# Tree attention on one core: the root part of V copied by GpSimd, loads ahead of stores in the DMA queue, the last pair split by heads

## The chip, the cores and the metric

One Trainium2 chip, one core of it. The metric is the device time of one execution in microseconds (us); lower is better. The kernel before was run three times: median 138.92 us, from 138.73 to 139.44.

## What is computed

Attention for 8 x 12 = 96 heads of 512 tokens and 64 dimensions, with a mask in which token i sees itself and its ancestors in a binary tree (the parent of i is (i - 1) // 2):

```python
mask = np.zeros((seq, seq))
for i in range(seq):
    mask[i, i] = 1
    parent = i
    while parent > 0:
        parent = (parent - 1) // 2
        mask[i, parent] = 1
scores = np.einsum('bhqd,bhkd->bhqk', Q, K) * scale
scores = scores + (1 - mask) * (-1e9)
weights = np.exp(scores - np.max(scores, axis=-1, keepdims=True))
weights = weights / (np.sum(weights, axis=-1, keepdims=True) + 1e-10)
return np.einsum('bhqk,bhkd->bhqd', weights, V).astype(np.float32)
```

Inputs and output are float32 in HBM, 12.6 MB each.

## The kernel before

The work is cut into 48 pairs of heads; pair i holds heads 2i and 2i + 1. Token 4p + t of a head lies on partition p, slot t, so a load puts 1 KB of each head on every partition, and the load itself turns float32 into bf16.

For each pair: `transpose` (L237) turns K and Q with 16 small TensorE operations into the PSUM tile `kqp` (one buffer, pool `psT`). `evac` (L250) copies it to SBUF on VectorE. `scores1` and `scores2` (L266, L288) write two groups of masked scores to PSUM (the first group holds keys near the root, the mask comes in through a matmul of codes), and ScalarE takes the exponential of each. `values` (L320) multiplies by V into the PSUM tile `ob`, with a column of ones for the sums of weights. `norm` (L345) takes reciprocals (L351) and multiplies (L352) on VectorE into the output tile `of`, one for two pairs (four heads).

`values` needs V in another order of nodes. So for each group o of 16 heads, V is copied from the loaded tile `vst` into one of two tiles `vt`, by three kinds of copies that all stand on L198: `spread_top` (nodes under 128, four copies, partitions 0 to 31 of the source), `spread_l7` (the next 128 nodes, four copies) and `spread_leaves` (the other 256, two). `vst` has three buffers of 16 heads, the tiles `kst` and `qst` have four buffers of 8 heads.

The order of the work is written out by hand; each engine runs its instructions in the order of the program. In loop step i come the scores of pair i, values and norm of pair i - 1, transposes and evacuation of pair i + 2, then `spread(i)` (L422), which deals out the copies of V, then `pool(i)` (L444). Copies of the first two groups are listed by step in `early` (L397); later groups follow a cycle of eight steps.

All loads and nearly all stores are issued by GpSimd (POOL), in one list, `pool_program` (L366). `pool(i)` takes operations from its front as long as `ready` (L386) lets them go, so a load that has to wait for a buffer holds up everything behind it. Each of these transfers uses one of eight semaphores in turn, so the ninth waits for the landing of the first. A whole transfer of 8 heads of one input is 512 KB on the chip, and so is a store of four heads. Of the copies of V, POOL makes `spread_top` of heads 0 to 7. The output of the last two pairs goes out by SyncE and ScalarE in three stores (L478 to L481).

At the start TensorE runs 21 matmuls on zeros (`fill`, L310), so that it is busy before the first data come.

Of the kernel before, what the change touches and what calls it, by code (L numbers as in the profile page):

```python
# [98 lines left out]
def kernel(  # L99
# [7 lines left out]
    nc = tc.nc  # L107
# [32 lines left out]
    opool = ctx.enter_context(tc.tile_pool(name="opool", bufs=14))  # L140
# [82 lines left out]
    def transpose_one(dst, i, a, t, units, st, perm):  # L223

        step = units[1] - units[0]
        if units[2] - units[1] == step:
            dst = dst[64 * a:64 * a + 64, units[0]:units[3] + 1:step, :]
        else:
            gap = units[2] - units[0]
            dst = dst[64 * a:64 * a + 64, units[0]:units[0] + 2 * gap, :].rearrange(  # L230
                "p (x y) c -> p x y c", x=2
            )[:, :, 0:2, :]
        nc.tensor.transpose(  # L233
            out=dst, in_=st[2 * i // KB][:, 2 * i % KB + a, t, :], identity=perm
        )
# [84 lines left out]
    def values(i):  # L320

        if i not in obs:
            obs[i] = psO.tile([P, 2, 512], fp32, name="ob")
        ob = obs[i]
        e1, e2, vt = ets[i], e2s[i % NE], vts[(2 * i // VB) % NV]

        def product(e, a, t, tile_v, lo=0, hi=128, **flags):
            nc.tensor.matmul(  # L328
                out=ob[lo:hi, a, 65 * t:65 * t + 65],
                lhsT=e[:, a, PLACE[t], lo:hi],  # L330
                rhs=vt[:, 2 * i % VB + a, tile_v, 0:D + 1],
                **flags,
            )

        for a in range(2):
            for t in range(4):
                product(e1, a, t, 0, start=t == 0, stop=False)
            for t in (2, 3):
                product(e2, a, t, 1 + t, start=False, stop=False)
        for a in range(2):  # L340
            for t in (0, 1):
                product(e2, a, t, 1 + SELF[t], 0, 64, start=False, stop=t == 1)
                product(e2, a, t, 1 + t, 64, 128, start=False, stop=t == 1)

    def norm(i):  # L345
        q, r = divmod(i, 2)
        if r == 0:
            ofs[q] = opool.tile([P, 4, 4, D], fp32, name="of")
        o4 = obs[i][:, :, 0:260].rearrange("p a (t c) -> p a t c", c=D + 1)
        rec = small.tile([P, 2, 4, 1], fp32, name="rec")  # L350
        nc.vector.reciprocal(out=rec[:, :, :, :], in_=o4[:, :, :, D:D + 1])  # L351
        nc.vector.tensor_tensor(  # L352
            out=ofs[q][:, 2 * r:2 * r + 2, :, :],
            in0=o4[:, :, :, 0:D],
            in1=rec[:, :, :, :].to_broadcast([P, 2, 4, D]),
            op=ALU.mult,
        )
# [8 lines left out]
    def pool_program():  # L366

        def tops(h0, h1):
            return [(spread_top, nc.gpsimd, j, 0, h0, h1) for j in range(4)]
# [5 lines left out]
        ops += [(load_v, 8, 8), (load_qk, 8, 4)] + tops(0, 4) + [(load_qk, 12, 4)] + tops(4, 8)  # L375
        ops += [(load_qk, 16, 8), (load_v, 16, 8), (load_v, 24, 8), (load_qk, 24, 8)]
        ops += [(load_v, 32, 8), (load_v, 40, 8), (load_qk, 32, 8)]
        ops += [(load_v, 48, 8), (load_v, 56, 8), (load_qk, 40, 8)]
        for g, qs in ((6, (0,)), (7, (1,)), (8, (2, 3)), (9, (4, 5))):
            ops += [(load_v, 8 * g + 16, 8), (load_qk, 8 * g, 8)] + stores(*qs)  # L380
        ops += [(load_qk, 80, 4)] + stores(6, 7) + [(load_qk, 84, 4)] + stores(8, 9)
        ops += [(load_qk, 88, 4)] + stores(10, 11, 12) + [(load_qk, 92, 2)] + stores(13, 14)
        ops += [(load_qk, 94, 2)] + stores(*range(15, NQ - 1))
        return ops

    def ready(op, i):  # L386
# [4 lines left out]
        if f is load_v:  # L391
            return i >= (-1, -1, -1, 3, 11, 15)[args[0] // VB]
        if f is spread_top:
            return True
        return 2 * i >= 4 * (args[1] + 1)

    def early(i):  # L397
# [3 lines left out]
        top = lambda ks, o, h0, h1: [(spread_top, v, k, o, h0, h1) for k in ks]  # L401
        leaf = lambda ks, o, h0, h1: [(spread_leaves, s, k, o, h0, h1) for k in ks]
        if i == 0:
            return l7(range(4), 0, 0, 4) + leaf((0, 1), 0, 0, 4)
        if i == 1:
            return l7(range(4), 0, 4, 8) + leaf((0, 1), 0, 4, 8)
        if i == 2:
            return top(range(4), 0, 8, 16)
        if i == 3:
            return l7(range(4), 0, 8, 16) + leaf((0, 1), 0, 8, 16)  # L410
        if i in (6, 7, 8):
            h = (0, 8)
        elif i in (9, 10, 11):
            h = (8, 16)
        else:
            return []
        n = i % 3
        return [top(range(3), 1, *h) + leaf((0,), 1, *h),
                top((3,), 1, *h) + l7((0, 1), 1, *h) + leaf((1,), 1, *h),
                l7((2, 3), 1, *h)][n]  # L420

    def spread(i):  # L422

        if i < 12:
            todo = early(i)
        else:
            v, s = nc.vector, nc.scalar
            o, k = divmod(i + 7, 8)
            if o < 2 or o >= NH // VB:
                todo = []  # L430
            else:
                top = [(spread_top, v, j) for j in range(4)]
                l7 = [(spread_l7, v, j) for j in range(4)]
                leaf = [(spread_leaves, v, 0)] + [(spread_leaves, s, 1, h, h + 8) for h in (0, 8)]
                todo = [top[:2], top[2:], leaf[:2], l7[:1], l7[1:2] + leaf[2:], l7[2:3], l7[3:], []]
                if o == 2:
                    todo = [[], [], [], top[:3], top[3:] + leaf[:2], l7[:2] + leaf[2:], l7[2:], []]
# [21 lines left out]
    fill(0, 4)  # L459
# [4 lines left out]
    for i in range(1, NP + 1):  # L464
# [3 lines left out]
        if i >= 2:  # L468
            values(i - 1)
            norm(i - 1)  # L470
# [41 lines left out]
```

## Time and profile before

| What | Value |
|---|---|
| median of three runs | 138.92 us |
| the profiled execution | 139.43 us |
| its span | 136.6 us |
| TensorE (PE) busy | 115.4 us, 85% |
| VectorE (DVE) busy | 108.1 us, 79% |
| ScalarE (ACT) busy | 100.9 us, 74% |
| GpSimd (POOL) busy | 62.7 us, 46% |
| DMA packets | 41737, 32.06 MB |

The profile shows one execution. Its page gives the busy time of each engine, the span in 40 equal slices of 3.4 us (a digit 9 is 90% or more; for the DMA it is the mean of 16 DMA engines), and the chain of work that ended last, followed back from the last instruction. The view of transfers gives, for the DMAs issued in a stretch, how long they took from issue to landing. The difference of 2.8 us between the execution's time and its span lies around the program.

### The profile page before, as it was taken

How to read it: one execution, taken by the hardware profiler on the slowest of the kernel's cores; microseconds unless marked ns; L12 is line 12 of the kernel's file. 1: busy time of each engine (PE TensorE's matmuls, PEld its weight loads, DVE VectorE, ACT ScalarE, POOL GpSimd, SP SyncE). 2: the span in 40 equal slices, each digit the busy share in tenths (PEclk: the TensorE clock that was granted, in tenths of full speed). 3: DMA queues.
4: the chain of work that ended last, by engine and by line, in shares of the span. 5: the costliest groups of instructions: out<-in, count | busy, mean ns of one | idle time of the engine just before them, and what ended most of it. 6: DMA issues, size and time to landing. Idle time of an engine off the chain costs nothing.

```text
span 136.6 us, 5453 instructions
## 1 busy us (share of the span) xinstructions
PE 115.4 (85%) x2420; PEld 79.6 (58%) x2421; DVE 108.1 (79%) x220; ACT 100.9 (74%) x116; POOL 62.7 (46%) x84
## 2 busy tenths in 40 slices
PE   6999867795998968779999999999998999879820
PEld 2345545573675646557676766666765667657510
DVE  3344997869879999989999899999899988665440
ACT  4083977659799898568997879996879977785900
POOL 6997987323420362342262253342446746644200
PEclk9999999999599999999999999999999999999995
DMA  3999999999999999999999999999999999999972
GB/s 88 143 156 193 197 196 201 194 200 196 197 198 198 198 199 199 197 198 197 276 201 200 279 198 225 326 204 212 333 299 278 330 281 359 337 354 404 354 303 91
DMA packets 41737, 32.06 MB, mean 235 GB/s; under 512 B 1226, under 2 KB 38730, under 8 KB 41714
## 3 DMA queue, kind: packets, MB, share of 16 engines
q0 software_dynamic: 40960, 30.94, 125.1%
q1 hardware_dynamic: 560, 0.56, 1.2%
q8 instruction: 18, 0.29, 0.8%
q10 hardware_dynamic: 194, 0.23, 0.6%
q14 instruction: 5, 0.04, 0.1%
HBM read 38.01 MB, written 12.58 MB: 370 GB/s over the span
## 4 chain that ended last, share of the span: by engine, by line
DMA 56%; PE 23%; POOL 6%; ACT 6%; issue 4%; DVE 1%; POOLq 0%; ACTq 0%
DMA vst<-in_V_dram 44%; DMA out_dram<-of 11%; PE ob L328 8%; PE kqp L233 5%; PE s L270 3%; PE s L293 3%; POOL kst L185 2%; ACT e L304 2%; POOL qst L185 2%; PE s L299 2%; PE s L275 2%; ACT e L281 2%; ACT vt L198 2%; POOL vt L198 1%; DVE of L352 1%
## 5 line engine op out<-in xcount | busy, mean ns | idle before, releaser
L281 ACT ACTIVATE e<-s 128x1024 bf16<-128x1024 f32 x48 | 49.1, 1024 | 25.8 <-PE s L275 25.2
L328 PE MATMUL ob<-vt,e 128*128 128x65 bf16 (+1 forms) x960 | 38.6, 198 | 6.9 <-DVE of L352 6.0
L328 PEld LDWEIGHTS <-e 128*128 128x128 bf16 (+1 forms) x960 | 30.5, 103 | 15.2 <-DVE of L352 6.5
L304 ACT ACTIVATE e<-s 128x768 bf16<-128x768 f32 x48 | 38.6, 804 | 0.0
L198 DVE COPY vt<-vst 32x1024 bf16<-32x1024 bf16 (+3 forms) x68 | 35.1, 516 | 3.2 <-DMA vst<-in_V_dram 1.9
L259 DVE COPY kq<-kqp 128x1024 bf16<-128x1024 bf16 x48 | 32.7, 682 | 4.9 <-PE kqp L233 4.9
L352 DVE TENSOR_TENSOR of<-ob,rec 128x512 f32<-128x512 f32 x48 | 33.2, 692 | 1.7
L360 POOL DMA_DIRECT2D out_dram<-of x23 | 18.3, 797 | 20.1 <-DVE of L352 8.1
L185 POOL DMA_DIRECT2D kst<-in_K_dram x18 | 15.0, 833 | 14.9 <-DMA kst<-in_K_dram 5.5
L270 PE MATMUL s<-ctile 40*128 40x512 bf16 x96 | 19.2, 394 | 2.9 <-ACT e L281 2.6
L233 PE MATMUL kqp<-ptile,kst 128*64 128x128 bf16 x384 | 19.4, 223 | 1.7 <-issue 0.9
L185 POOL DMA_DIRECT2D qst<-in_Q_dram x18 | 15.1, 839 | 12.3 <-PE kqp L233 3.9
L233 PE MATMUL kqp<-ptile,qst 128*64 128x128 bf16 x384 | 19.5, 223 | 0.8 <-DMA qst<-in_Q_dram 0.8
L299 PEld LDWEIGHTS <-kq 64*128 64x128 bf16 x384 | 14.5, 94 | 8.8 <-issue 1.0
L185 POOL DMA_DIRECT2D vst<-in_V_dram x13 | 11.4, 882 | 17.8 <-DVE rec L351 6.6
L275 PE MATMUL s<-kq 64*128 64x512 bf16 x96 | 18.7, 383 | 1.0 <-DVE kq L259 1.0
L351 DVE RECIPROCAL rec<-ob 128x8 f32<-128x8 f32 x48 | 9.9, 205 | 12.1 <-PE ob L328 11.4
L293 PE MATMUL s<-ctile 40*128 40x480 bf16 x96 | 17.9, 368 | 0.8 <-ACT e L304 0.3
L198 ACT COPY vt<-vst 64x1024 bf16<-64x1024 bf16 (+1 forms) x18 | 17.0, 946 | 1.7 <-DMA vst<-in_V_dram 1.4
L299 PE MATMUL s<-kq 64*128 64x64 bf16 (+1 forms) x384 | 17.7, 209 | 0.4 <-issue 0.4
L233 PEld LDWEIGHTS <-kst 128*64 128x64 bf16 x384 | 12.8, 112 | 3.3 <-issue 2.4
L233 PEld LDWEIGHTS <-qst 128*64 128x64 bf16 x384 | 13.9, 113 | 1.2 <-DMA qst<-in_Q_dram 1.0
(17 smaller groups left out, 32.8 us busy)
## 6 DMA issues: line engine op xcount, KB each, us to landing
out_dram<-of POOLq DMA_DIRECT2D x23, 512.0 KB, 9.8
vst<-in_V_dram POOLq DMA_DIRECT2D x11, 512.0 KB, 19.0
kst<-in_K_dram POOLq DMA_DIRECT2D x8, 512.0 KB, 18.4
qst<-in_Q_dram POOLq DMA_DIRECT2D x8, 512.0 KB, 19.2
kst<-in_K_dram POOLq DMA_DIRECT2D x6, 256.0 KB, 10.4
qst<-in_Q_dram POOLq DMA_DIRECT2D x6, 256.0 KB, 10.4
kst<-in_K_dram POOLq DMA_DIRECT2D x4, 128.0 KB, 7.5
qst<-in_Q_dram POOLq DMA_DIRECT2D x4, 128.0 KB, 7.1
```

The lines of the kernel that those rows point to most:

```text
L185: nc.gpsimd.dma_start(out=kept[b][:, h0 % size:h0 % size + n, :, :].rearrange("p h t d -> p h (t d)"), in_=src[:, h0:h0 + n, :],)
L198: (eng.copy if eng is nc.scalar else eng.tensor_copy)(out=out, in_=in_)
L233: nc.tensor.transpose(out=dst, in_=st[2 * i // KB][:, 2 * i % KB + a, t, :], identity=perm)
L259: nc.vector.tensor_copy(out=kq[:, :, :, :].rearrange("p k (x y) c -> p k x y c", y=2), in_=src)
L270: nc.tensor.matmul(out=sp[:, a, :], lhsT=k1code[64 * a:64 * a + BITS, :], rhs=q1code[64 * a:64 * a + BITS, :], start=True, stop=False,)
L275: nc.tensor.matmul(out=sp[:, a, :], lhsT=keys(i, a, TOP), rhs=qTs[i][64 * a:64 * a + 64, :, :].rearrange("p t c -> p (t c)"), start=False, ...
L281: nc.scalar.activation(out=et[:, :, :, :].rearrange("p a t c -> p (a t c)"), in_=sp[:, :, :].rearrange("p a c -> p (a c)"), func=AF.Exp, s ...
L293: nc.tensor.matmul(out=flat[:, a, 32:512], lhsT=k2code[64 * a:64 * a + BITS, :], rhs=q2code[64 * a:64 * a + BITS, 32:512], start=True, sto ...
L299: nc.tensor.matmul(out=flat[:, a, lo:hi], lhsT=keys(i, a, TILE2[t]), rhs=qTs[i][64 * a:64 * a + 64, :, :].rearrange("p t c -> p (t c)")[:, ...
L304: nc.scalar.activation(out=e2s[i % NE][:, :, :, 32:128].rearrange("p a t c -> p (a t) c"), in_=sp[:, :, :, 32:128].rearrange("p a t c -> p ...
L328: nc.tensor.matmul(out=ob[lo:hi, a, 65 * t:65 * t + 65], lhsT=e[:, a, PLACE[t], lo:hi], rhs=vt[:, 2 * i % VB + a, tile_v, 0:D + 1], **flags,)
L352: nc.vector.tensor_tensor(out=ofs[q][:, 2 * r:2 * r + 2, :, :], in0=o4[:, :, :, 0:D], in1=rec[:, :, :, :].to_broadcast([P, 2, 4, D]), op=A ...
```

## The change

- GpSimd makes all copies of kind `spread_top`, for all six groups of 16 heads; VectorE makes none. They stand in POOL's list between loads: 28 copies more there (12 of 8 heads, 16 of 16 heads), 28 fewer on VectorE.
- VectorE's other copies of V in the first three groups come mostly one or two in a step, where two to four came together.
- K and Q of heads 8 to 11 (the fifth and sixth pair) are loaded ahead of V of heads 8 to 15, behind POOL's first four copies.
- The stores move towards the end of POOL's list: six stand ahead of the last load instead of fifteen. Output tiles `of`: 18 buffers for 14. Two loads of V become ready one step later.
- The last pair's values are written to the buffer of `kqp` instead of `ob`, all products of one head before those of the other, and its norm is done by heads.
- The four `fill` matmuls between the second pair's transposes and the first values go.
- In `transpose_one` a slice is taken in two steps; the addresses are the same.

The diff, without that last part and the removed call `fill(0, 4)`:

```diff
     work = ctx.enter_context(tc.tile_pool(name="work", bufs=4))
     etpool = ctx.enter_context(tc.tile_pool(name="etpool", bufs=3))
     small = ctx.enter_context(tc.tile_pool(name="small", bufs=4))
-    opool = ctx.enter_context(tc.tile_pool(name="opool", bufs=14))
+    opool = ctx.enter_context(tc.tile_pool(name="opool", bufs=18))
     psS = ctx.enter_context(tc.tile_pool(name="psS", bufs=1, space=bass.MemoryType.PSUM))
     psT = ctx.enter_context(tc.tile_pool(name="psT", bufs=1, space=bass.MemoryType.PSUM))
     psO = ctx.enter_context(tc.tile_pool(name="psO", bufs=1, space=bass.MemoryType.PSUM))
...
 
     def values(i):
 
-        if i not in obs:
+        if i == NP - 1:
+            obs[i] = psT.tile([P, 2, 512], fp32, name="kqp")
+        elif i not in obs:
             obs[i] = psO.tile([P, 2, 512], fp32, name="ob")
         ob = obs[i]
         e1, e2, vt = ets[i], e2s[i % NE], vts[(2 * i // VB) % NV]
...
                 **flags,
             )
 
-        for a in range(2):
+        def first(a):
             for t in range(4):
                 product(e1, a, t, 0, start=t == 0, stop=False)
             for t in (2, 3):
                 product(e2, a, t, 1 + t, start=False, stop=False)
-        for a in range(2):
+
+        def second(a):
             for t in (0, 1):
                 product(e2, a, t, 1 + SELF[t], 0, 64, start=False, stop=t == 1)
                 product(e2, a, t, 1 + t, 64, 128, start=False, stop=t == 1)
 
-    def norm(i):
+        order = (first, second) * 2 if i == NP - 1 else (first, first, second, second)
+        for n, part in enumerate(order):
+            part(n // 2 if i == NP - 1 else n % 2)
+
+    def norm(i, heads=((0, 2),)):
         q, r = divmod(i, 2)
         if r == 0:
             ofs[q] = opool.tile([P, 4, 4, D], fp32, name="of")
-        o4 = obs[i][:, :, 0:260].rearrange("p a (t c) -> p a t c", c=D + 1)
-        rec = small.tile([P, 2, 4, 1], fp32, name="rec")
-        nc.vector.reciprocal(out=rec[:, :, :, :], in_=o4[:, :, :, D:D + 1])
-        nc.vector.tensor_tensor(
-            out=ofs[q][:, 2 * r:2 * r + 2, :, :],
-            in0=o4[:, :, :, 0:D],
-            in1=rec[:, :, :, :].to_broadcast([P, 2, 4, D]),
-            op=ALU.mult,
-        )
+        for a0, a1 in heads:
+            o4 = obs[i][:, a0:a1, 0:260].rearrange("p a (t c) -> p a t c", c=D + 1)
+            rec = small.tile([P, a1 - a0, 4, 1], fp32, name="rec")
+            nc.vector.reciprocal(out=rec[:, :, :, :], in_=o4[:, :, :, D:D + 1])
+            nc.vector.tensor_tensor(
+                out=ofs[q][:, 2 * r + a0:2 * r + a1, :, :],
+                in0=o4[:, :, :, 0:D],
+                in1=rec[:, :, :, :].to_broadcast([P, a1 - a0, 4, D]),
+                op=ALU.mult,
+            )
 
     def store(eng, q, h0=0, n=4):
         eng.dma_start(
...
 
     def pool_program():
 
-        def tops(h0, h1):
-            return [(spread_top, nc.gpsimd, j, 0, h0, h1) for j in range(4)]
+        def tops(h0, h1, o=0):
+            return [(spread_top, nc.gpsimd, j, o, h0, h1) for j in range(4)]
 
         def stores(*qs):
             return [(store, nc.gpsimd, q) for q in qs]
 
         ops = [(load_qk, 0, 2), (load_v, 0, 4), (load_qk, 2, 2), (load_qk, 4, 4), (load_v, 4, 4)]
-        ops += [(load_v, 8, 8), (load_qk, 8, 4)] + tops(0, 4) + [(load_qk, 12, 4)] + tops(4, 8)
-        ops += [(load_qk, 16, 8), (load_v, 16, 8), (load_v, 24, 8), (load_qk, 24, 8)]
-        ops += [(load_v, 32, 8), (load_v, 40, 8), (load_qk, 32, 8)]
-        ops += [(load_v, 48, 8), (load_v, 56, 8), (load_qk, 40, 8)]
-        for g, qs in ((6, (0,)), (7, (1,)), (8, (2, 3)), (9, (4, 5))):
-            ops += [(load_v, 8 * g + 16, 8), (load_qk, 8 * g, 8)] + stores(*qs)
-        ops += [(load_qk, 80, 4)] + stores(6, 7) + [(load_qk, 84, 4)] + stores(8, 9)
-        ops += [(load_qk, 88, 4)] + stores(10, 11, 12) + [(load_qk, 92, 2)] + stores(13, 14)
-        ops += [(load_qk, 94, 2)] + stores(*range(15, NQ - 1))
+        ops += tops(0, 4) + [(load_qk, 8, 4), (load_v, 8, 8)] + tops(4, 8) + [(load_qk, 12, 4)]
+        ops += [(load_qk, 16, 8), (load_v, 16, 8), (load_v, 24, 8)] + tops(8, 16)
+        ops += [(load_qk, 24, 8), (load_v, 32, 8), (load_v, 40, 8), (load_qk, 32, 8)]
+        ops += tops(0, 8, 1) + [(load_v, 48, 8)] + tops(8, 16, 1)
+        ops += [(load_v, 56, 8), (load_qk, 40, 8)] + tops(0, 16, 2)
+        for g, qs in ((6, ()), (7, ()), (8, (0,)), (9, (1,))):
+            ops += [(load_v, 8 * g + 16, 8)] + (tops(0, 16, 4) if g == 9 else [])
+            ops += [(load_qk, 8 * g, 8)] + stores(*qs) + (tops(0, 16, 3) if g == 7 else [])
+        ops += [(load_qk, 80, 4)] + stores(2) + [(load_qk, 84, 4)] + stores(3)
+        ops += [(load_qk, 88, 4)] + tops(0, 16, 5) + stores(4) + [(load_qk, 92, 2)] + stores(5)
+        ops += [(load_qk, 94, 2)] + stores(*range(6, NQ - 1))
         return ops
 
     def ready(op, i):
...
         if f is load_qk:
             return i >= 4 * (args[0] // KB) - 15
         if f is load_v:
-            return i >= (-1, -1, -1, 3, 11, 15)[args[0] // VB]
+            return i >= (-1, -1, -1, 4, 11, 16)[args[0] // VB]
         if f is spread_top:
-            return True
+            return args[2] < 2 or i >= 8 * (args[2] - 1)
         return 2 * i >= 4 * (args[1] + 1)
 
     def early(i):
 
         v, s = nc.vector, nc.scalar
         l7 = lambda ks, o, h0, h1: [(spread_l7, v, k, o, h0, h1) for k in ks]
-        top = lambda ks, o, h0, h1: [(spread_top, v, k, o, h0, h1) for k in ks]
         leaf = lambda ks, o, h0, h1: [(spread_leaves, s, k, o, h0, h1) for k in ks]
-        if i == 0:
-            return l7(range(4), 0, 0, 4) + leaf((0, 1), 0, 0, 4)
-        if i == 1:
-            return l7(range(4), 0, 4, 8) + leaf((0, 1), 0, 4, 8)
-        if i == 2:
-            return top(range(4), 0, 8, 16)
-        if i == 3:
-            return l7(range(4), 0, 8, 16) + leaf((0, 1), 0, 8, 16)
-        if i in (6, 7, 8):
-            h = (0, 8)
-        elif i in (9, 10, 11):
-            h = (8, 16)
-        else:
-            return []
-        n = i % 3
-        return [top(range(3), 1, *h) + leaf((0,), 1, *h),
-                top((3,), 1, *h) + l7((0, 1), 1, *h) + leaf((1,), 1, *h),
-                l7((2, 3), 1, *h)][n]
+        return {
+            0: l7(range(4), 0, 0, 4) + leaf((0, 1), 0, 0, 4),
+            1: l7(range(4), 0, 4, 8) + leaf((0, 1), 0, 4, 8),
+            3: l7((0, 1), 0, 8, 16) + leaf((0,), 0, 8, 16),
+            4: l7((2, 3), 0, 8, 16) + leaf((1,), 0, 8, 16),
+            6: l7((0, 1), 1, 0, 8) + leaf((0,), 1, 0, 8),
+            7: l7((2, 3), 1, 0, 8) + leaf((1,), 1, 0, 8),
+            8: l7((0,), 1, 8, 16),
+            9: l7((1,), 1, 8, 16) + leaf((0,), 1, 8, 16),
+            10: l7((2,), 1, 8, 16),
+            11: l7((3,), 1, 8, 16) + leaf((1,), 1, 8, 16),
+            12: l7((0,), 2, 0, 16),
+            13: l7((1,), 2, 0, 16) + leaf((1,), 2, 0, 8),
+            14: l7((2,), 2, 0, 16),
+            15: l7((3,), 2, 0, 16) + leaf((1,), 2, 8, 16),
+            16: [(spread_leaves, v, 0, 2, 0, 16)],
+        }.get(i, [])
 
     def spread(i):
 
-        if i < 12:
+        if i < 17:
             todo = early(i)
         else:
             v, s = nc.vector, nc.scalar
             o, k = divmod(i + 7, 8)
-            if o < 2 or o >= NH // VB:
+            if o >= NH // VB:
                 todo = []
             else:
-                top = [(spread_top, v, j) for j in range(4)]
                 l7 = [(spread_l7, v, j) for j in range(4)]
                 leaf = [(spread_leaves, v, 0)] + [(spread_leaves, s, 1, h, h + 8) for h in (0, 8)]
-                todo = [top[:2], top[2:], leaf[:2], l7[:1], l7[1:2] + leaf[2:], l7[2:3], l7[3:], []]
-                if o == 2:
-                    todo = [[], [], [], top[:3], top[3:] + leaf[:2], l7[:2] + leaf[2:], l7[2:], []]
+                todo = [[], [], leaf[:2], l7[:1], l7[1:2] + leaf[2:], l7[2:3], l7[3:], []]
                 todo = [op[:3] + (o,) + (op[3:] or (0, VB)) for op in todo[k]]
         for op in todo:
             op[0](*op[1:])
...
     scores2(0)
     fill(0, 8)
     transpose(1)
-    fill(0, 4)
     spread(0)
     evac(1)
     values(0)
...
             scores2(i)
         if i >= 2:
             values(i - 1)
-            norm(i - 1)
+            norm(i - 1, ((0, 1), (1, 2)) if i == NP else ((0, 2),))
         for n in AHEAD.get(i, (i + 2,)):
             if n < NP:
                 transpose(n)
```

More of the change, by code (lines that the diff above doesn't have):

```diff
@@ L223, in transpose_one @@
     def transpose_one(dst, i, a, t, units, st, perm):
+        dst = dst[64 * a:64 * a + 64, :, :]
         step = units[1] - units[0]
         if units[2] - units[1] == step:
-            dst = dst[64 * a:64 * a + 64, units[0]:units[3] + 1:step, :]
+            dst = dst[:, units[0]:units[3] + 1:step, :]
         else:
             gap = units[2] - units[0]
-            dst = dst[64 * a:64 * a + 64, units[0]:units[0] + 2 * gap, :].rearrange(
+            dst = dst[:, units[0]:units[0] + 2 * gap, :].rearrange(
                 "p (x y) c -> p x y c", x=2
```

## Prediction

> **What bounds the kernel now.** I read the page's slices first, then the chain that ended last, then the landings of single transfers, and only then the engines.
>
> ```profile
> span 136.6 us, 5453 instructions
> ...
> DMA  3999999999999999999999999999999999999972
> GB/s 88 143 156 193 197 196 201 194 200 196 197 198 198 198 199 199 197 198 197 276 201 200 279 198 225 326 204 212 333 299 278 330 281 359 337 354 404 354 303 91
> ...
> DMA 56%; PE 23%; POOL 6%; ACT 6%; issue 4%; DVE 1%; POOLq 0%; ACTq 0%
> ```
>
> No engine is above 85%, but the DMA is at nine tenths or more in 37 of 40 slices, and the chain lies 56% in it. While only loads run, it stands at 198 GB/s (written side: a load halves its bytes from f32 to bf16); where only stores run, near 400. The view of transfers says so for 24 to 64 us, and for 124 to 128.5 us:
>
> ```profile
> DMA packets 15497, 7.91 MB, mean 198 GB/s; under 512 B 235, under 2 KB 15490, under 8 KB 15490
> ```
> ```profile
> DMA packets 491, 1.80 MB, mean 400 GB/s; under 512 B 55, under 2 KB 55, under 8 KB 490
> ```
>
> So a load of 512 KB costs 0.524 MB / 198 GB/s = 2.65 us, a store of 512 KB 1.31 us. Are these times serial, one after another? The chain of waits in order of time (start, duration) answers:
>
> ```profile
> 31.31 20.66 DMA vst<-in_V_dram
> 51.97 0.60 issue
> 52.57 19.25 DMA vst<-in_V_dram
> ```
>
> The first lands at 51.97, the second at 71.82. Between them stand six more loads and one store: 7 x 2.65 + 1.31 = 19.86; seen, 19.85. It is one queue without a hole. It stays so to the end: the store issued at 124.04 takes 9.0 us to land, the one issued at 128.55 (4.5 us later) takes 5.8:
>
> ```profile
> out_dram<-of POOLq DMA_DIRECT2D x1, 512.0 KB, 9.0
> ```
> ```profile
> q0 software_dynamic: 53, 0.18, 78.8%
> ...
> out_dram<-of POOLq DMA_DIRECT2D x1, 512.0 KB, 5.8
> ```
>
> They land at 133.0 and 134.35, 1.3 apart: one store's service. Yet in that window (128.6 to 129.2) the queue holds only 78.8% of the 16 engines. So some of the 16 are idle while at least one is still working off its backlog, and a landing waits for that slowest one. The last output, issued at 132.30, lands 3.3 us later, at 135.6; the span ends 1.0 after it.
>
> The whole sum: the eighth load lands at 13.68 (issued 6.46, 7.22 in the chain). Behind it come 33 loads' worth (of 36) and 24 stores: 33 x 2.65 + 24 x 1.31 = 118.9, so 132.6; seen 135.6. The 3.0 us over are lost in two stretches: 1.2 before 51.97 (14 loads, 37.1, would give 50.8), 1.9 after 71.82 (12 loads and 23 stores, 61.9, would give 133.7). Compute ends at 132.27 and needs 3.3 for its last store: 135.6 too. **Two chains end together**; shortening compute alone frees nothing.
>
> **The change, part by part.**
>
> *Tops to GpSimd.* VectorE loses 28 copies: 16 of 32x1024 and 12 of 32x512; where POOL is quiet they take 0.42 (two in 0.85 at 45.31) and 0.29 us (three in 0.88 at 30.76), so about 10 us of its 108.1 goes. POOL gains the same 28. Its only row is smaller:
>
> ```profile
> L198 POOL COPY vt<-vst x8: 387/396/435, 9.6 to 15.1; 32x256 bf16<-32x256 bf16 x8
> ```
>
> For 32x1024 the ends are 0.40 (all fixed) and 4 x 0.396 = 1.58 (all per element). A POOL MEMSET of one element takes 0.10; with that as the fixed part, 0.10 + 4 x 0.296 = 1.28, which I take (0.69 for 32x512). Sum on POOL: 16 x 1.28 + 12 x 0.69 = 29 us (11 to 35) on 62.7 busy of 136.6: room in total, but each group holds up the transfers queued behind it.
>
> *What waits behind the copies.* POOL may have eight transfers out; each needs the landing of the eighth before. The tight place is the last group (heads 80 to 95), put between Q of 88 and store 4. Q of 88 may go when store 1 has landed; then the DMA holds six loads of 256 KB and two stores: 6 x 1.325 + 2 x 1.31 = 10.6 us. POOL spends 0.76 on that issue, then four copies, then issues store 4, whose first data need up to 2.7 us (the first load, 128 KB, takes 3.4 to land less 0.66 of service). Left for the copies: 7.1 us, **1.78 each**. At 1.28 there is 2.0 us to spare, at 1.58 0.8. The group before it (heads 64 to 79) waits for pair 23's values (76.1 at the old pace) while the DMA has work to 13.68 + 20 x 2.65 + 1.2 + 19.86 = 87.7: 2.2 each. The earlier groups have over 10 us of queue in front. So the DMA doesn't run dry: cost nothing, up to the price in rival C.
>
> *The shared path.* Alone, VectorE's 32x512 copies take 0.29 each; beside POOL copies 0.37:
>
> ```profile
> 30.76 0.88 DVE L198 COPY vt<-vst 32x512 bf16<-32x512 bf16 x3 [0.54 <-DMA vst<-in_V_dram]
> ```
> ```profile
> 14.44 1.49 DVE L198 COPY vt<-vst 32x512 bf16<-32x512 bf16 x4
> ```
>
> A longer POOL copy can hold one up longer: bounds 0 and 1.28 each. Two or three VectorE copies meet each group of four: at half a copy, 3 x 0.64 x 5 groups = 10 us, about what VectorE saves. This lies on compute, which has cover (below).
> The Trainium skill speaks against this part: "SBUF — State Buffer", section "Who interferes with whom", says that VectorE in a two-port mode and GpSimd exclude each other, and that the later one "fully blocks". By the page each VectorE copy that meets a POOL copy can pay all of it, 15 x 1.28 = 19 us at worst as an estimate; by the rows, where a copy pays 0.08 on the mean, 15 x 0.08 = 1 us.
>
> *K, Q of 8 to 11 ahead of V of 8 to 15.* The same bytes in the first eleven transfers; the queue's sum is unchanged. Pair 4's K and Q come one V load (2.65 us) earlier, V later by two half loads (2.65): its copies end near 20.1 + 4 x 0.69 = 23, before values(4), which now run near 25.8 (pair 4's reciprocal at 26.58 less 0.79 of matmuls). POOL's first copies no longer stand behind three issues, and four `fill` matmuls (0.81 us) go: values(0) start up to 1 us sooner. None of this shortens the queue.
>
> *Later stores.* The same 24 stores; only six stand ahead of the last load instead of fifteen. Last K/Q land at 13.68 + 87.5 + 6 x 1.31 + 1.2 to 3.1 = 110 to 112, not at 115.1 + 8.8 = 123.9. Seventeen POOL stores then follow, 22 us of service, all long computed, or computed faster (4.4 us per two pairs) than their place in that backlog needs. Behind them: nothing but the end.
>
> *Last pair.* Values no longer wait for VectorE's norm of the pair before (1.12 us of idle PE at 130.52), and the norm goes by heads, at two more small VectorE operations. Compute: K/Q of heads 72 to 79 land near 94 (before 97.9); pair 36's exponential came 4.8 after them, so 98.8; eleven periods of 2.11 to 2.3 and 4.2 for the end: 126 to 128.5, less 0.6. That is 4 us sooner than 132.3, and 3 to 5 us under the queue's end, which is the cover for VectorE's new waits.
>
> **Sum.** The queue carries the same bytes in the same service times, starts as before (the first eight transfers are identical) and loses what it lost before: last landing 135.6, span 136.6. The profiled execution took 139.43, 0.5 above the median of 138.92; I forecast no change on that median: **138.9**, own range 138.2 to 139.6. What the change gives back on compute, the DMA keeps.
>
> **Rivals.**
>
> *B, faster.* The 3.0 us over are not fixed to one engine: a different order loses one of the losses of about 1.1 (137.8), or all (135.9; compute, 130 to 132 with its last store, would allow that). For it: the losses are jumps, not a rate, and engines are idle at 128.6 to 129.2. Against it: the early stretch is identical, and the landings at 133.0 and 134.35 show that the slow engine does not catch up when others are idle.
>
> *C, slower.* POOL's copies block the DMA. Place: the last group, before store 4; decides from 1.78 us a copy. If each copy also waits out one VectorE copy (0.69): 1.58 + 0.69 = 2.27, four times 0.49 = 2.0 us, so 140.9. For it: both rows above show that the two engines delay each other, and 32x1024 on POOL is in no trace here. Against it: POOL's own copies beside VectorE's took 387 to 397 ns, as little as alone.
>
> *Not what it says.* The order of POOL's queue is written out by hand and the built program keeps it, so the stores are later; I give this no chance of its own.
>
> **Numbers.** Forecast 0.53, B 0.25, C 0.22. Faster by over 0.5% 0.25, within 0.5% 0.53, slower 0.22; 0.5% (0.7 us) is about what a measurement of this kernel tells from no change. Low 136.9 leaves the deeper half of B out, high 140.9 takes C's worked price.
>
> **What would show it.** Right: DMA slices full to the last but one; store landings 1.3 apart to the end; last K/Q landing near 111; the last VectorE row near 128, over 5 us before the last landing. B: last landing under 135. C: POOL copies over 1.8 us, and slices under nine tenths near 95 to 108. Wrong altogether: VectorE's copies held up so long that compute ends after 132.3.

## The result, and the profile after

The changed kernel takes 139.97 us (median of 20 runs, 138.99 to 141.08) where the kernel before takes 139.03 (20 runs, 138.30 to 140.43). The ratio is 1.0061, with a 95% interval of 1.0037 to 1.0084. The forecast was no change at 138.9; the kernel is 0.6% slower. The time lies above the forecast's own range (138.2 to 139.6) and inside the whole one (136.9 to 140.9); the forecast said no change, and the kernel got slower.

The page of the kernel after; the lines answer to those shown of before:

```profile
span 136.7 us, 5449 instructions
...
DMA  3999999999999999999999999999999999999993
GB/s 85 143 154 198 181 190 172 198 198 198 199 197 198 199 199 198 201 195 201 195 199 197 198 197 276 202 203 277 274 270 258 286 361 398 405 396 399 397 367 126
...
PE 34%; DMA 21%; DVE 19%; ACT 13%; issue 6%; POOL 4%; ACTq 0%; POOLq 0%
```

The DMA is full to the last slice but one, as the forecast asked. But the fifth to seventh slices (13.7 to 24 us) move 181, 190 and 172 GB/s where the kernel before moved 197, 196 and 201: the queue is short there. The pure stores near 400 begin at slice 34, because they come later. The chain now runs mostly through compute (PE, DVE and ACT have 66% of it, the DMA 21%), since compute did not get out of the queue's way: its last VectorE operation ends at 133.15, after the 132.27 of before, and the last landing is at 135.77 after 135.63.

This profiled execution has the shortest span of the kernel's runs, and it is the only one with more than 2.0 us around the span (3.2): it is not typical. Over the timed runs the mean span is 138.0 us, against 136.3 for the kernel before. What lies around the span went the other way: 1.9 us on the mean, against 2.55. Both numbers are needed below, so the table has them for every run. A few executions, of whatever kernel, fall into a slower state; the ratios and means leave them out.

| kernel | ratio to before | 95% interval | mean span us | around it us |
|---|---|---|---|---|
| before | 1 | | 136.3 | 2.55 |
| after | 1.0061 | 1.0037 to 1.0084 | 138.0 | 1.9 |
| e1, later stores | 1.0081 | 1.0051 to 1.0110 | 137.4 | 2.4 |
| e16, the same again | 1.0035 | 1.0001 to 1.0069 | 137.0 | 2.5 |
| e2, root copies on GpSimd | 1.0004 | 0.9982 to 1.0026 | 136.3 | 2.5 |
| e3, order of the start, no `fill(0, 4)` | 1.0067 | 1.0024 to 1.0111 | 137.5 | 2.4 |
| e4, last pair | 0.9947 | 0.9918 to 0.9976 | 136.2 | 2.0 |
| e5, order of the start alone | 1.0075 | 1.0045 to 1.0105 | 137.6 | 2.6 |
| e6, no `fill(0, 4)` alone | 0.9989 | 0.9962 to 1.0016 | 136.4 | 2.4 |
| e7, after, lighter TensorE | 1.0076 | 1.0051 to 1.0102 | 138.2 | 1.8 |
| e8, after, lighter stores | 0.9749 | 0.9716 to 0.9781 | 133.6 | 1.85 |
| e9, e2 and e4 together | 0.9994 | 0.9970 to 1.0017 | 136.8 | 1.9 |
| e10, after, old start | 1.0016 | 0.9982 to 1.0050 | 137.0 | 2.0 |
| e11, K, Q first, issued early | 1.0006 | 0.9976 to 1.0035 | 136.4 | 2.5 |
| e12, old order, issued late | 1.0119 | 1.0090 to 1.0148 | 137.9 | 2.6 |
| e13, e1 with lighter TensorE | 0.9974 | 0.9944 to 1.0005 | 137.0 | 1.8 |
| e14, e1 and e2 together | 1.0030 | 1.0012 to 1.0048 | 136.7 | 2.5 |
| e15, after, K, Q first, issued early | 1.0003 | 0.9978 to 1.0028 | 136.9 | 2.0 |

### The profile page after: what moved, and what is told of

It reads as the page before. It is cut to its first block, busy times and chain, and to the rows that moved or that the text cites. A ratio compares the mean times of both kernels' runs of the same rounds, so it can differ in the third digit from the quotient of the medians.

```text
span 136.7 us, 5449 instructions
## 1 busy us (share of the span) xinstructions
PE 116.2 (85%) x2417; PEld 80.5 (59%) x2417; DVE 101.5 (74%) x194; ACT 101.3 (74%) x116; POOL 87.4 (64%) x112
## 4 chain that ended last, share of the span: by engine, by line
PE 34%; DMA 21%; DVE 19%; ACT 13%; issue 6%; POOL 4%; ACTq 0%; POOLq 0%
DMA qst<-in_Q_dram 16%; PE ob L331 12%; DVE vt L198 8%; PE kqp L234 6%; DVE of L361 6%; DMA vst<-in_V_dram 6%; ACT e L305 5%; ACT e L282 5%; PE s L271 4%; DVE kq L260 4%; PE s L294 4%; PE s L276 3%; PE s L300 3%; ACT vt L198 3%; DVE rec L360 2%
## 5 line engine op out<-in xcount | busy, mean ns | idle before, releaser
L331 PEld LDWEIGHTS <-e 128*128 128x128 bf16 (+1 forms) x960 | 31.3, 104 | 14.0 <-issue 5.9
L198 POOL COPY vt<-vst 32x1024 bf16<-32x1024 bf16 (+2 forms) x36 | 29.0, 806 | 13.3 <-DMA vst<-in_V_dram 7.6
L361 DVE TENSOR_TENSOR of<-ob,rec 128x512 f32<-128x512 f32 x47 | 32.5, 692 | 1.6
L198 DVE COPY vt<-vst 32x2048 bf16<-32x2048 bf16 (+3 forms) x40 | 27.6, 690 | 2.9 <-DMA vst<-in_V_dram 1.7
L185 POOL DMA_DIRECT2D qst<-in_Q_dram x18 | 14.6, 811 | 7.5 <-PE s L276 4.0
```

Source lines behind the costliest of these rows:

```text
L185: nc.gpsimd.dma_start(out=kept[b][:, h0 % size:h0 % size + n, :, :].rearrange("p h t d -> p h (t d)"), in_=src[:, h0:h0 + n, :],)
L198: (eng.copy if eng is nc.scalar else eng.tensor_copy)(out=out, in_=in_)
L331: nc.tensor.matmul(out=ob[lo:hi, a, 65 * t:65 * t + 65], lhsT=e[:, a, PLACE[t], lo:hi], rhs=vt[:, 2 * i % VB + a, tile_v, 0:D + 1], **flags,)
L361: nc.vector.tensor_tensor(out=ofs[q][:, 2 * r + a0:2 * r + a1, :, :], in0=o4[:, :, :, 0:D], in1=rec[:, :, :, :].to_broadcast([P, a1 - a0, ...
```

## The experiments

**One part at a time.** The first four runs put one part of the change each into the kernel before.

e1, the stores:

```diff
-opool = ... bufs=14
+opool = ... bufs=18
-for g, qs in ((6, (0,)), (7, (1,)), (8, (2, 3)), (9, (4, 5))):
+for g, qs in ((6, ()), (7, ()), (8, (0,)), (9, (1,))):
...
-... stores(6, 7) ... stores(8, 9) ... stores(10, 11, 12) ... stores(13, 14) ... stores(*range(15, NQ - 1))
+... stores(2) ... stores(3) ... stores(4) ... stores(5) ... stores(*range(6, NQ - 1))
```

> The kernel before with only the stores moved later in POOL's list (and 18 output tiles). Queue theory (the slowest DMA engine carries the same bytes, nothing else counts): ratio 1.000, within 0.3%. Fetch theory (TensorE's instruction blocks come over the same DMA engines, and a backlog of stores that is always eight deep at the end delays the blocks of the last two pairs): 1.005 to 1.010, with idle of TensorE that no instruction ends of 1 us or more near the end. Lock theory (GpSimd's copies delay VectorE): 1.000.

Measured: 1.0081, a number of the fetch theory, and its sign is there: at 123.06 TensorE waits 1.42 us for nothing that the profile shows (0.87 at the same place before). But the profiled execution (136.8) is one of the shorter ones; the spans lie loosely in two groups, 136.3 to 137.3 and 137.6 to 138.7. It has its last load at 111.29, and its last landing at 135.88, only 0.25 later than before. So this kernel is slower, and what its slower executions lose, its profile does not show.

e2, the copies:

```diff
+def tops(h0, h1, o=0): ... nc.gpsimd ...
-28 spread_top copies in early() and spread() on VectorE
+the same 28 in pool_program(), in the groups of the changed kernel;
+VectorE's other copies and the readiness of the loads as there
```

> The kernel before with only the root copies moved to GpSimd and VectorE's other copies dealt as in the changed kernel. Queue theory: 1.000, within 0.3%. Fetch theory: 1.000. Lock theory: 1.004 to 1.010, with VectorE's 32x2048 copies at 0.8 us or more instead of 0.69.

Measured: 1.0004. VectorE's copies of 32x2048 do take longer (0.79 us on the mean), but compute ends at 131.05, 1.2 us sooner, and the last landing is at 135.58, where it was. Shortening compute frees nothing, and 28 copies more on GpSimd cost nothing.

e3, the start:

```diff
-ops += [(load_v, 8, 8), (load_qk, 8, 4)] + tops(0, 4) + [(load_qk, 12, 4)] + tops(4, 8)
+ops += tops(0, 4) + [(load_qk, 8, 4), (load_v, 8, 8)] + tops(4, 8) + [(load_qk, 12, 4)]
...
-fill(0, 4)
```

> The kernel before with only K and Q of heads 8 to 11 ahead of V of heads 8 to 15, POOL's first copies ahead of both, and without the four matmuls on zeros. Queue theory: 1.000, or up to 1.004 if three transfers issued 3 us later leave the DMA engines short between 14 and 18 us. Fetch and lock theory: 1.000.

Measured: 1.0067. The two edits were then parted.

e4, the last pair:

```diff
+if i == NP - 1:
+    obs[i] = psT.tile([P, 2, 512], fp32, name="kqp")
...
+order = (first, second) * 2 if i == NP - 1 else (first, first, second, second)
...
+norm(i - 1, ((0, 1), (1, 2)) if i == NP else ((0, 2),))
```

> The kernel before with only the last pair's values in the transposes' PSUM buffer, one head after the other, with the norm by heads. Queue theory: 1.000, because the last landing is the queue's; compute ends about 0.8 us sooner (131.5). Theory that compute's end sets the time: 0.994.

Measured: 0.9947, faster than both kernels, by its interval. The number is that of the theory that compute's end sets the time. But compute ends at 132.21, where it did, and the span is what it was (136.2): the whole gain lies around it, 2.0 us for 2.55. The transfers after the last engine event show a difference there. Of the kernel before, from 136.6 to 140 us, and of e4, from 136.2 to 140:

```profile
DMA packets 1, 0.02 MB, mean 5 GB/s; under 512 B 0, under 2 KB 0, under 8 KB 0
...
q8 instruction: 1, 0.02, 2.4%
```
```profile
DMA packets 0, 0.00 MB, mean 0 GB/s; under 512 B 0, under 2 KB 0, under 8 KB 0
```

Before fetches one more block of instructions after its last engine has stopped; e4 fetched it at 132.1, inside the span. Over the 18 profiles of this study the two go together: where the packet comes after the span, the profiled execution has 2.4 to 3.2 us around its span; where it is inside or missing, 1.7 to 2.1. Why e4 fetches earlier was not found.

e5 and e6, the two edits of e3 apart:

```diff
e5: the order of the first issues as in e3, fill(0, 4) kept
e6: the order as before, fill(0, 4) gone
```

> The kernel before with only the order at the start changed: POOL's first copies, then K and Q of heads 8 to 11, then V of heads 8 to 15; all matmuls on zeros kept. If the order costs the time of the start's experiment: 1.005 to 1.009. If the missing matmuls on zeros cost it (eight TensorE instructions fewer, so that every later block of 256 instructions is cut at another place): 1.000.

> The kernel before without the four matmuls on zeros, the order of loads kept. If the cut of TensorE's instruction blocks counts: 1.005 to 1.009. If the order of the loads counts: 1.000, at the most 0.3% either way.

Measured: 1.0075 and 0.9989. It is the order, and it is the part of the change that the forecast had called free.

**Is it the queue or compute?** Both these kernels are the changed one with something left out.

```diff
e7: for pairs 40 to 47
-for t in (2, 3): product(e2, ...)
+for t in (): ...
-for t in (0, 1): product(e2, ...)
+for t in (): ...
e8: in store()
+n = 2 if 8 <= q < 16 else n
```

e7 leaves out the second weight group's part of the values of pairs 40 to 47; e8 leaves half of stores 8 to 15 unwritten, 8 x 0.655 = 5.2 us of the queue.

> The changed kernel with the products of the second group of weights left out for pairs 40 to 47 (12 of 20 matmuls of each; the output of these heads is then not the reference's). TensorE is some 3 us lighter at the end, the DMA queue is the same. Queue theory: the ratio stays near 1.006. Fetch theory (compute's end, delayed by late instruction blocks, sets the time): 0.995 to 1.000.

> The changed kernel that stores only two of the four heads in the eight stores 8 to 15 (the rest of these heads is not written): 2 MB less, 5.2 us of the queue. Queue theory: compute's end plus 3 us is the next bound, so 0.995 to 1.000. Fetch theory: compute's end is already the bound, so it stays near 1.006, or falls a little because blocks come sooner; landings of the last POOL store near 130.

Measured: 1.0076 and 0.9749. The last VectorE operation of e7, and the issues of its last stores with the us to their landing (SyncE's last one and ScalarE's):

```profile
127.73 0.42 DVE L361 TENSOR_TENSOR of<-kqp,rec 128x256 f32<-128x256 f32 x1
```
```profile
out_dram<-of SPq DMA_DIRECT2D x1, 256.0 KB, 8.6
out_dram<-of SPq DMA_DIRECT2D x1, 128.0 KB, 8.7
out_dram<-of ACTq DMA_DIRECT2D x1, 128.0 KB, 7.0
```

Compute is done at 128.15, 5 us sooner than in the changed kernel, and the time is the same: the last stores wait 7 to 8.7 us in the queue (2.6 to 3.6 in the changed kernel). Taking 5.2 us of stores away gives 1.0061 - 0.9749 = 3.1%, 4.3 us, more than either theory had forecast; compute ends sooner there too, at 130.65, so it is e7 that parts the two. The queue bounds the changed kernel; the rival that VectorE's waits bound it fails.

This holds to about half a microsecond, as e7 ends in another way than the changed kernel. GpSimd's last store, issued at 125.30, is the last of all to land, at 136.51. GpSimd closes the program with a DRAIN, and in all 18 traces this ends 0.8 to 0.9 us after the landing of GpSimd's own last store. In e7 it therefore ends the span, 1.7 us after the last landing, where the changed kernel takes 0.9. With 0.9 the queue of e7 would give a span of 137.4, so up to 0.6 us of the changed kernel's 138.0 may still be compute's. These are the drains of the kernel before, of e7 and of e13 (below): the third number is the longest in ns, the next one its start.

```profile
L507 POOLq DRAIN  x3: 51/93/6610, 128.5 to 136.3; - x3
```
```profile
L512 POOLq DRAIN  x3: 51/98/12132, 125.3 to 137.9; - x3
```
```profile
L507 POOLq DRAIN  x3: 51/101/11264, 125.2 to 137.0; - x3
```

**What the order does to the queue.** POOL in the kernel before, from its eighth issue on:

```profile
6.46 1.67 POOL L185 DMA_DIRECT2D vst<-in_V_dram  x2
8.07 0.81 POOL L185 DMA_DIRECT2D kst<-in_K_dram  x1
8.85 0.77 POOL L185 DMA_DIRECT2D qst<-in_Q_dram  x1
9.59 1.75 POOL L198 COPY vt<-vst 32x256 bf16<-32x256 bf16 x4
11.29 0.75 POOL L185 DMA_DIRECT2D kst<-in_K_dram  x1
```

and after:

```profile
6.44 0.80 POOL L185 DMA_DIRECT2D vst<-in_V_dram  x1
8.69 1.81 POOL L198 COPY vt<-vst 32x256 bf16<-32x256 bf16 x4 [1.45 <-DMA vst<-in_V_dram]
10.45 0.74 POOL L185 DMA_DIRECT2D kst<-in_K_dram  x1
11.18 0.76 POOL L185 DMA_DIRECT2D qst<-in_Q_dram  x1
11.91 0.91 POOL L185 DMA_DIRECT2D vst<-in_V_dram  x1
14.03 1.81 POOL L198 COPY vt<-vst 32x256 bf16<-32x256 bf16 x4 [1.21 <-DMA vst<-in_V_dram]
15.79 0.76 POOL L185 DMA_DIRECT2D kst<-in_K_dram  x1
```

Before, K of heads 8 to 11 is issued at 8.07, and K of 12 to 15 at 11.29. After, POOL reaches its four copies sooner, but they wait for V (1.45 us idle), and all that stands behind them waits too: the two K's are issued at 10.45 and 15.79, 2.4 and 4.5 us later. Two theories were left. The starved queue: the issues come too late to keep the 16 engines fed. The late V: pair 4's values wait for V, which comes after K and Q, and compute never makes that up. They part when the order and the lateness of the issues are changed separately.

```diff
e11, before with
+ops += [(load_qk, 8, 4), (load_v, 8, 8)] + tops(0, 4) + [(load_qk, 12, 4)] + tops(4, 8)
e12, before with
+ops += tops(0, 4) + [(load_v, 8, 8), (load_qk, 8, 4)] + tops(4, 8) + [(load_qk, 12, 4)]
e10, after with before's line:
+ops += [(load_v, 8, 8), (load_qk, 8, 4)] + tops(0, 4) + [(load_qk, 12, 4)] + tops(4, 8)
e15, after with e11's line
```

> The kernel before with K and Q of heads 8 to 11 ahead of V of heads 8 to 15, but all three still issued ahead of GpSimd's first four copies. Theory of the starved queue (the cost of the start's order lies in the four copies, which wait for V and stand ahead of the issues, so that too little is queued between 12 and 24 us): 1.000, 195 to 200 GB/s in that stretch. Rival, the late V (pair 4's values wait for V that lands two half loads later, and the later pairs never make that up): 1.0075 as with the whole order.

> The kernel before with GpSimd's first four copies ahead of the issues of V of heads 8 to 15 and of K and Q of heads 8 to 11, in the old order of the loads. Theory of the starved queue: 1.005 to 1.0075, with 170 to 190 GB/s between 12 and 24 us. Rival, the late V: V is issued at most 2.4 us later and lands about as before; 1.000 to 1.002.

> The changed kernel with the order of the first issues as before (V of heads 8 to 15, then K and Q of heads 8 to 11, both ahead of GpSimd's first four copies). If the two causes add up, 1.0061 / 1.0075 = 0.999 of the time before, and between 12 and 24 us the queue moves 195 to 200 GB/s again in place of 170 to 190. Rival: the later stores alone hold the changed kernel up, whatever the start; then 1.006 to 1.008.

> The changed kernel with its K, Q ahead of V, but with these three issues ahead of GpSimd's first four copies. Starved queue: as with the old start, 0.999 to 1.002 of the time before, and 195 to 200 GB/s between 12 and 24 us. If the order of the loads itself costs it: 1.006.

Measured: 1.0006, 1.0119, 1.0016, 1.0003. The stretch from 12 to 24 us, the last column being GB/s: before, after, e11, e12 and e15 in turn.

```profile
core 0: us, PE busy (x) PEld busy (x) DVE busy (x) ACT busy (x) POOL busy (x), PEclk, DMA share, GB/s
12.00:24.00 12.00, 9.22 (x204) 6.39 (x200) 9.91 (x21) 9.62 (x12) 9.44 (x14) 1.00 1.45 197
```
```profile
12.00:24.00 12.00, 9.35 (x206) 6.43 (x202) 8.40 (x17) 9.74 (x12) 10.50 (x16) 1.00 1.40 184
```
```profile
12.00:24.00 12.00, 7.44 (x163) 5.18 (x161) 7.87 (x17) 8.24 (x10) 9.70 (x14) 0.98 1.45 197
```
```profile
12.00:24.00 12.00, 8.99 (x160) 5.75 (x157) 9.59 (x20) 8.80 (x11) 10.00 (x15) 0.90 1.39 183
```
```profile
12.00:24.00 12.00, 9.63 (x210) 6.73 (x208) 8.54 (x17) 9.16 (x12) 10.42 (x17) 1.00 1.45 197
```

Where the copies stand ahead of the issues, the queue moves less: 184 GB/s after, 183 in e12, 182 in e7, and 188 and 193 in e5 and e3, where the loss is smaller. Where the issues stand ahead, it moves 195 to 197 (196 in e10), in either order of the loads. 13 GB/s over 12 us are 156 KB, 0.8 us of the queue. In e12 this stays to the end: V of heads 24 to 31 lands 0.83 later than before (34.27), GpSimd's last store 0.75 later (135.07). The mean spans agree: 138.0 after, 136.9 with the issues ahead (e15), the same K, Q and V in the same order; and 1.2 to 1.6 us over before in e3, e5 and e12. e12's 1.0119 is above its forecast, and what these spans lose beyond 0.8 us is not explained. The late V is not it: in e11 V of heads 8 to 15 lands at 19.83 (after 19.51, before 17.47), and that costs nothing.

A rival is that late loads make compute late, and compute the last stores. e7 and e13 (below) exclude it as the whole cause: compute ends at 128.15 and 128.50 in them, too early to matter, and both have the later stores. e7 has the new start and a mean span of 138.2, e13 the old one and 137.0. The last landing is at 136.51 in the one and 135.71 in the other, 0.8 apart, and the 0.8 is there from the start: V of heads 24 to 31 lands at 34.00 and 33.15. They also differ in the copies on GpSimd and in the last pair, which lengthened no span one by one (e2, e4) and 0.5 us together (e9, below).

The loss is not beyond recovery. In the changed kernel's profiled execution GpSimd's fifth store lands 0.63 later than in e15, its last one only 0.16; that is how this execution's last landing (135.77) comes so near that of before.

**The later stores and the sum of the parts.** e9 is e2 and e4 in one kernel:

```diff
+both the copies of e2 and the last pair of e4, on the kernel before
```

> The kernel before with two of the changed kernel's parts: the root copies on GpSimd with VectorE's copies dealt singly, and the last pair's values in the transposes' PSUM with the norm by heads; order of the first loads and places of the stores as before. If the parts add up, 0.9947 x 1.0004 = 0.995 of the time before, and its last landing stays within 0.6 us of the 135.6 of before (the queue is the bound). Rival: the tail's gain hangs on where an instruction packet falls in that one program; then this program, whose instructions stand elsewhere, is at 1.000.

Measured: 0.9994, not the 0.995 of the sum but the rival's number. Its reason is not the rival's: around the span the kernel keeps e4's gain (1.9), but the span is 0.5 longer, for a reason that the runs don't show. So e4 is the only version that beats both kernels, and what it wins lies around its span.

For the stores, compute was shortened behind them:

```diff
e13: e1 with e7's cut of the products (pairs 40 to 47)
e14: e1's stores and e2's copies, on the kernel before
e16: e1's kernel once more
```

> The kernel before with the later stores alone, and without the products of the second weight group of pairs 40 to 47 (that part of the values is left out), so that compute ends about 5 us sooner. If the later stores cost their 0.8% in the queue itself, 1.006 to 1.010 as with all products. If they cost it because compute then ends too late for its last stores (fed sooner, throttled, stalled by an instruction block), 1.000 or less.

> The kernel before with the later stores and the root copies on GpSimd (which end compute 1.2 us sooner at no cost in time). Queue: 1.008. Late compute: 1.000 to 1.003.

> A second profile of the kernel before with the later stores: its times fall in two groups (spans of 136.3 to 137.3 and of 137.6 to 138.7). If this one falls in the upper group, its trace shows whether the queue or compute ends late: a last landing more than 2.5 us after the last VectorE operation and landings of stores over 1.31 us apart speak for the queue, a last VectorE operation after 134 for compute.

Measured: 0.9974, 1.0030, 1.0035. The first two are what late compute forecast, and not the queue. The mean spans seem to say otherwise: 137.0 for e13, whose compute ends at 128.50, 0.7 above before, and 136.7 for e14. But e13's last landing is at 135.71, where before has 135.63; its span is longer behind that, because GpSimd's last store lands at 135.56 (134.32 before) and the DRAIN shown above then ends the span. e14's last landing is at 135.89. So no more than 0.3 us of the later stores' cost is shown to lie in the queue.

That e1 measured 1.1 us of span is not explained, nor did e16's profile (span 136.7, last landing 135.71) fall into the upper group that it was to show. The times give one clue: the five longest spans of e1 and e16 (138.1 to 138.9) are the executions with 1.7 or 1.8 us around the span, and all others have 2.3 to 3.0. In this kernel the two go against each other; no profile was taken of such an execution.

## Why the prediction was wrong, and where it was right

**The step that failed** is the one on K, Q of 8 to 11: "The same bytes in the first eleven transfers; the queue's sum is unchanged", with "POOL's first copies no longer stand behind three issues" counted as a gain, and the sum's "starts as before". The bytes are the same, but three issues now stand behind the copies, and the copies wait for V. The forecast saw which instructions moved and priced only the side that moved up. "The earlier groups have over 10 us of queue in front" does not hold for the first group: when K of heads 8 to 11 is issued at 10.45, all that was issued ahead of it has landed by 13.98. The queue falls from 197 to 184 GB/s between 12 and 24 us, 0.8 us of its work, and the order as a whole costs 1.1 us of span (138.0 after, 136.9 in e15), more than the 0.9 us that the kernel lost. With the issues ahead again (e15) the changed kernel is at 1.0003: what was forecast for the whole holds for the rest of it.

**"Loses what it lost before"** was the second fault: the 3.0 us over were carried along as a constant. They are not: in e7, where compute is out of the way, the last landing is at 136.51, 3.9 over the same sum of 132.6. Rival B had this right as a mechanism and wrong in sign: a different order can lose more as well as less.

**Later stores: "Behind them: nothing but the end."** The loads came forward as forecast (last K, Q at 112.17; 110 to 112 was said). Yet the later stores alone were slower, at 1.0081 and, repeated, 1.0035. With compute shortened they cost nothing (e13, 0.9974), so little of it lies in the queue; where it does lie stays open.

**Time around the span** was taken as fixed. It fell by 0.6 us, as in e4, and hid that much of the loss: 1.7 us of span became about 1 us of time.

**The bound** was right: e7 shows that the queue sets the time, e8 agrees, and e2 shows that shortening compute alone frees nothing.

**POOL's copies** were priced a little high. Groups by form, after:

```profile
L198 POOL COPY vt<-vst 32x1024 bf16<-32x1024 bf16 x16 | 17.6, 1098 | 9.2 <-PE ob L331 4.3 <-DMA vst<-in_V_dram 4.1
...
L198 POOL COPY vt<-vst 32x512 bf16<-32x512 bf16 x12 | 8.1, 671 | 1.3 <-DMA vst<-in_V_dram 0.8
```

1.10 and 0.67 us, against 1.28 and 0.69, and 25.7 us for the 28 copies, against 29. Rival C's 1.78 a copy was not reached, and its place before store 4 shows no thin slice. But its kind of loss is the one that came: GpSimd's copies hold back the DMA. They do so at the start and not in the last group, and by waiting for data and not by their length.

**Compute was wrong**: 133.15, not 126 to 128.5, and later than the 132.3 that the forecast gave as the sign of being wrong altogether. Part of this is the start's order again: with the issues ahead, e15 ends compute at 131.93. And the forecast took TensorE to be waiting for K and Q: pair 36's first exponential was to start 4.8 us after its K and Q land, but they land at 94.54 (97.91 before) and it starts at 101.92 (102.70 before). VectorE lost 28 copies but only 6.6 us (108.1 to 101.5), not 10, as those that stayed became slower. The same 16 copies, before and after:

```profile
L198 DVE COPY vt<-vst 32x2048 bf16<-32x2048 bf16 x16 | 11.4, 712 | 0.5
```
```profile
L198 DVE COPY vt<-vst 32x2048 bf16<-32x2048 bf16 x16 | 13.5, 844 | 0.5
```

0.13 us more each on the mean, but it is not spread evenly. Ten of the 16 take 0.68 to 0.75 us. Three meet copies of POOL, at 46.26, 48.73 and 74.39, and take 0.93, 0.99 and 1.55; three more, of 0.90 to 1.15, met none and ran while GpSimd issued a DMA, as some of the ten did too. The longest, and the two POOL copies that it meets:

```profile
74.39 1.55 DVE L198 COPY vt<-vst 32x2048 bf16<-32x2048 bf16 x1
```
```profile
74.36 2.48 POOL L198 COPY vt<-vst 32x1024 bf16<-32x1024 bf16 x2 [4.33 <-PE ob L331]
```

The first POOL copy takes 1.03 us and ends at 75.39, VectorE's ends 0.55 later, and the second POOL copy, which starts meanwhile, takes 1.40. In the other two as well VectorE's copy ends 0.54 to 0.55 us after the POOL copy that was running when it started. So these rows agree with the Trainium skill ("SBUF — State Buffer", section "Who interferes with whom") that the later of two such copies "fully blocks": it pays what is left of the copy ahead of it. The forecast's 1 us from the rows was too low and its 19 us by the page too high: VectorE gained about 3.4 us less than the 10, as only three of these 16 copies met one of POOL's. This does not make compute late, as e2, with the same copies on GpSimd, ends it at 131.05.

Part of the rest is idle time of TensorE that no faster VectorE can shorten. After, at 122.69:

```profile
122.69 0.30 PE L234 MATMUL kqp<-ptile,kst 128*64 128x128 bf16 x4 [1.42 <-issue]
```

It waited 1.42 us for nothing that the profile shows (0.87 at the same place before), and 1.25 more at 130.26. As compute sets at most some tenths of the time (e7), this wrong step did the forecast's time little harm.

## What to carry to other kernels

When work is moved ahead of a DMA issue on the engine that issues it, price what the issue then waits for: a copy that waits for data holds back every transfer behind it, and where the queue bounds the kernel, an early gap (here 0.8 us out of 12) can stay to the last landing, as in e12. Read GB/s by slices, and not the busy tenths: the tenths stayed at 9 while the rate fell from 197 to 184. And keep the span apart from the time around it, since an edit near the end can move one without the other, and by as much as the effect that is looked for.

## What the runs showed of the hardware beyond the forecast

The time around the span goes with one fetch of instructions: 2.4 to 3.2 us where a packet of 16 KB comes after the last engine's end, 1.7 to 2.1 where it does not. That the one causes the other is inferred from the 18 profiles; no run moved the packet alone.

The span can end with GpSimd and not with the last landing: its closing DRAIN ended 0.8 to 0.9 us after the landing of its own last store in all 18 traces, and in e7 and e13, where that store landed last or nearly so, it put 0.6 to 0.8 us on the span.

TensorE's clock falls after a pause. In e5 it stood idle for 4.13 us before 23.80; the windows from 20 to 30 us give the granted clock in the third column from the end:

```profile
20.00:22.00 2.00, 0.00 (x0) 0.00 (x0) 1.64 (x4) 1.66 (x2) 2.00 (x4) 0.93 1.38 176
22.00:24.00 2.00, 0.20 (x5) 0.19 (x6) 1.69 (x4) 0.43 (x1) 2.00 (x3) 0.50 1.41 191
24.00:26.00 2.00, 2.00 (x22) 1.06 (x20) 1.06 (x2) 0.06 (x1) 0.42 (x1) 0.50 1.46 196
26.00:28.00 2.00, 2.00 (x40) 1.71 (x38) 1.78 (x5) 1.66 (x2) 1.00 (x1) 0.50 1.46 198
28.00:30.00 2.00, 2.00 (x42) 1.34 (x39) 1.30 (x2) 0.76 (x1) 0.50 (x1) 0.87 1.46 198
```

Its last matmul before the pause ends at 19.67; half speed begins at about 21.7, 2.0 us later, and lasts to 28.5, 4.7 us into the work that follows. The stretch at half speed is thus 6.8 us long. Cut into pieces of 3.41 us, it and the time before it look like this:

```profile
18.30:21.71 3.41, 1.37 (x46) 1.12 (x41) 1.36 (x3) 3.00 (x4) 3.41 (x4) 1.00 1.41 183
21.71:25.12 3.41, 1.32 (x18) 0.95 (x19) 2.18 (x6) 0.72 (x1) 2.71 (x4) 0.50 1.42 190
25.12:28.53 3.41, 3.41 (x51) 2.38 (x48) 3.13 (x7) 1.73 (x2) 1.00 (x1) 0.50 1.45 197
```

The Trainium skill ("TensorE: Matmul & The Clock Gate", section "Part 1: The HAM clock gate") describes a free-running window of about 3.4 us, half speed after an idle one and full speed after a busy one. The length of two windows agrees with it, and so does full speed after the third piece, in which TensorE was busy throughout. The step down does not quite: the first piece still holds 1.37 us of matmuls, so the window need not be idle.

The 4.7 us of work at half speed cost at most about 2.4 us, an estimate from these windows. In this execution compute ends at 135.51, 3.2 us later than before, and there it, and not the queue, sets the end. A late V need not cost that: e11 has a pause of 3.31 us at the same place and a stretch at half speed, its compute ends at 132.86, and its ratio is 1.0006.
